# Moving the split weight buffers to other addresses in SBUF (a two-stage transformer layer in fp32r matmuls)

## The chip, the core and the metric

The kernel runs on one core of a Trainium2 chip. The metric is device time in microseconds (us), the median of three runs. Lengths of single instructions are given in nanoseconds (ns).

## What is computed

The reference is one layer of a hybrid encoder on an input of 256 tokens by 2048 features, in float32:

```python
u = rmsnorm(x, norm_mix_g)
z = u @ w_in                      # 2048 x 5140, four head groups
y = concat(gated_conv, pooling, gated_linear_attention, forgetting_attention)(z)
x = x + y @ w_out                 # 2048 x 2048
u = rmsnorm(x, norm_ffn_g)
x = x + (silu(u @ w_gate) * (u @ w_up)) @ w_down   # 2048 x 5632 twice, 5632 x 2048
```

The weights amount to some 50 million float32 numbers, each used once per run of the kernel.

## The kernel before

**Precision.** Each float32 operand is split into a high part, which is the value rounded to the format fp32r, and a low part, which is the rest. A product is then the sum of three: high times high, high times low and low times high. The activations u (for both norms), y (mixer output) and hT (hidden layer, 44 blocks of 128 features) are held in SBUF as such pairs, `u[:, k, 0]` the high and `u[:, k, 1]` the low part, 256 tokens each.

**Weights.** All big weights are packed into 384 chunks `wall[i]` of 128 partitions by 1024 columns (512 KB). `stage_through` (L104) brings a chunk from memory into one of four `raw` buffers, ScalarE rounds it into `hi` (L114) and VectorE subtracts to get `lo` (L115). There are four hi and four lo buffers, hi0 to hi3 and lo0 to lo3, and chunk i uses number i modulo 4. Chunks are prepared three ahead of the one in use (`LOOK`).

**Products.** Most chunks are used by `block_fm` (L136): 317 chunks, in which the weight is the stationary operand (128 by 128) and the activation is the moving one. Per chunk it does eight matmuls at L150 with `hi`, which stream both parts of the activation (512 columns), and eight at L155 with `lo`, which stream only the high part (256 columns). Eight matmuls alternate between two PSUM banks. In the last chunk of a block the eight of L155 come before the eight of L150. The first part of the program uses `block_lead` (L176, 256 columns at a time) and `block_tm` (L193), in which the weight chunk is the moving operand (512 columns) and the activation the stationary one. The last block (L159 to L171, `tail`) streams 256 columns per matmul.

**Order of the stages.** First 16 chunks in `block_lead` and `block_tm` for 40 chunks, until 163 us; then u times w_in by `block_fm` until 264 us; y times w_out until 353 us; gate and up projections (44 blocks of four chunks, so chunk 0 of a block always uses hi0 and lo0) until 843 us; then hT times w_down (eight blocks of eleven chunks, so that the buffer number and the place in the block are not tied), the eighth being the tail from 1056 us.

**Addresses.** Buffers lie in SBUF one behind the other, in the order in which the pools first see them. u begins at byte 32,896 of a partition. In what follows a buffer's *distance* is its address less that of u, modulo 512 bytes. A chunk buffer holds 4,096 bytes, but is allocated with 4,160 (`1040` columns, of which 1,024 are used), so each of the eight lies 64 bytes further on:

| buffer | hi0 | lo0 | hi1 | lo1 | hi2 | lo2 | hi3 | lo3 |
|---|---|---|---|---|---|---|---|---|
| distance from u before, bytes | 0 | 64 | 128 | 192 | 256 | 320 | 384 | 448 |

y and hT (which takes y's place later) begin at 125,568, a distance of 0 from u. Inside all these tensors each 128 by 128 weight begins at a multiple of 512 bytes and each activation part at a multiple of 1,024, so the distance holds for every matmul that pairs them.

Of the kernel before, what the change touches and what calls it, by code (L numbers as in the profile page):

```python
# [9 lines left out]
F32 = mybir.dt.float32  # L10
BF16 = mybir.dt.bfloat16
F32R = mybir.dt.float32r
# [5 lines left out]
P = 128  # L18
# [40 lines left out]
def trunk_kernel(ctx: ExitStack, tc: tile.TileContext, a, out):  # L59
# [4 lines left out]
    wpool = ctx.enter_context(tc.tile_pool(name="wpool", bufs=4))  # L64
    ev = ctx.enter_context(tc.tile_pool(name="ev", bufs=2))
# [31 lines left out]
    ones = con[:, C_ONE:C_ONE + P]  # L97


    staged = {}  # L100
    issued = [0]
    total = a["wall"].shape[0]

    def stage_through(n, ahead=AHEAD, parts=1):  # L104
        while issued[0] <= min(n, total - 1):
            i = issued[0]
            raw = wpool.tile([P, 1024], F32, name="raw", bufs=4)

            hi, lo = [wpool.tile([P, 1040], F32R, name=f"{v}{i % 4}", bufs=1)[:, :1024] for v in ("hi", "lo")]
            with tc.high_priority(offset=ahead):  # L110
                for q in range(parts):
                    c = slice(q * 1024 // parts, (q + 1) * 1024 // parts)
                    nc.sync.dma_start(out=raw[:, c], in_=a["wall"][i][:, c])
                    S.copy(out=hi[:, c], in_=raw[:, c])  # L114
                    V.tensor_tensor(out=lo[:, c], in0=raw[:, c], in1=hi[:, c].bitcast(F32), op=ALU.subtract)  # L115
            staged[i] = (hi, lo)
            issued[0] += 1
# [12 lines left out]
    def next_chunk():  # L130
        i = used[0]
        used[0] += 1
        stage_through(i + LOOK)
        return staged.pop(i)
# [91 lines left out]

    def rsqrt_of(dst, src, pool, mul, n):

        w = pool.tile([P, 64 if pool is ev else 3 * n], F32, name=f"rs{n}")
        v, r, q = [w[:, i * n:(i + 1) * n] for i in range(3)]  # L230
        V.tensor_scalar(out=v, in0=src, scalar1=mul, scalar2=EPS, op0=ALU.mult, op1=ALU.add)
        S.activation(out=r, in_=v, func=AF.Sqrt)
        V.reciprocal(out=r, in_=r)
        V.tensor_tensor(out=q, in0=r, in1=r, op=ALU.mult)
        V.scalar_tensor_tensor(out=q, in0=q, scalar=-0.5, in1=v, op0=ALU.mult, op1=ALU.mult)
        V.scalar_tensor_tensor(out=dst, in0=q, scalar=1.5, in1=r, op0=ALU.add, op1=ALU.mult)

    def token_rstd(sq):


        ps = misc()
        for t in range(2):
            PE.matmul(ps[:, t:t + 1], lhsT=sq[:, t * P:(t + 1) * P], rhs=con[:, C_ONE:C_ONE + 1], start=True, stop=True)
        rsqrt_of(rcol, ps[:, 0:2], ev, 1.0 / D, 2)
        yield
        yield
        ps2 = misc()
        for t in range(2):
            dg = ev.tile([P, P], F32, name="dg", bufs=1)
            V.tensor_scalar(out=dg, in0=ident, scalar1=rcol[:, t:t + 1], scalar2=None, op0=ALU.mult)  # L250
            PE.matmul(ps2[:, t * P:(t + 1) * P], lhsT=ones, rhs=dg, start=True, stop=True)
        S.copy(out=rb, in_=ps2[:, :T])
        yield
# [19 lines left out]
    for j in range(KT // 2):  # L273
        for ks in (slice(0, 1), slice(1, 2)) if j == 0 else (slice(2 * j, 2 * j + 2),):
            nc.sync.dma_start(out=xT[:, ks], in_=a["xT"][:, ks])
            if ks.start == 0:
                stage_through(0, 0, 2)
            for k in range(ks.start, ks.stop):
                split_u(k)
        stage_through(j, 0, 2)  # L280
# [187 lines left out]
    def gla_out(gv, sgg):  # L468
        ob = k4.tile([P, 2, 4, P], F32, name="ob", tag="k4")
        ss = mx.tile([P, 8], F32, name="gss")  # L470
        for t in range(2):
# [11 lines left out]
            yield  # L483
        rs = mx.tile([P, 8], F32, name="grs")
        rsqrt_of(rs, ss, mx, 1.0 / P, 8)
        for _ in range(8):
            yield
# [17 lines left out]
    def fox_qk(qk, qkT):  # L505

        ss = mx.tile([P, 16], F32, name="fss")
        for i in range(4):
            head_rstd(ss[:, 4 * i:4 * i + 4], qk[i // 2][:, i % 2].rearrange("p (h d) -> p h d", h=4), 4)
            yield  # L510
        rs = mx.tile([P, 16], F32, name="frs")
        rsqrt_of(rs, ss, mx, 1.0 / P, 16)
        for _ in range(3):
            yield
        for i in range(2):
            qn = k4.tile([P, 8, P], F32, name="qn", tag="k4")
            V.tensor_tensor(out=qn, in0=qk[i].rearrange("p t (h d) -> p (t h) d", h=4),
                            in1=rs[:, 8 * i:8 * i + 8, None].broadcast_to([P, 8, P]), op=ALU.mult)
            yield
            yield  # L520
            yield
            qT = k4.tile([P, 4, T], F32, name="qT", tag="k4")
            g = par[:, P_FQG + i:P_FQG + i + 1]
            for h in range(4):
                ps = misc()
                for t in range(2):
                    PE.transpose(out=ps[:, t * P:(t + 1) * P], in_=qn[:, t * 4 + h], identity=ident)
                if i == 0:
                    V.tensor_scalar(out=qT[:, h], in0=ps[:, :T], scalar1=g, scalar2=float(P) ** -0.5,
                                    op0=ALU.mult, op1=ALU.mult)  # L530
                else:
                    S.activation(out=qT[:, h], in_=ps[:, :T], func=AF.Copy, scale=g)
                yield
            qkT.append(qT)
# [175 lines left out]
    for j in range(2):  # L710
# [3 lines left out]
        for m in range(2):  # L714
            i = 2 * j + m
# [7 lines left out]
    for j in range(KT // 2):  # L723
        b = block_fm(y, order)
        for m in range(2):
            i = 2 * j + m
# [32 lines left out]
    for j in range(KT // 2):  # L759
        tail = j == KT // 2 - 1  # L760
        b = block_fm(hT, list(range(FT)), tail=tail)
        for m in range(2):
            i = 2 * j + m
# [65 lines left out]
```

## Time and profile before

| | us |
|---|---|
| median of three runs | 1093.26 (1093.09 to 1093.45) |
| the profiled execution's own time | 1092.44 |
| its span, first to last instruction | 1090.3 |
| TensorE matmul busy | 1084.9 |
| VectorE busy | 707.6 |
| ScalarE busy | 519.8 |

The profile's page gives busy times, a chain of the work that ended last, and groups of instructions. [...] What counts for the time is the spacing from one start to the next.

### The profile page before, as it was taken

How to read it: one execution, taken by the hardware profiler on the slowest of the kernel's cores; microseconds unless marked ns; L12 is line 12 of the kernel's file. 1: busy time of each engine (PE TensorE's matmuls, PEld its weight loads, DVE VectorE, ACT ScalarE, POOL GpSimd, SP SyncE). 2: the span in 40 equal slices, each digit the busy share in tenths (PEclk: the TensorE clock that was granted, in tenths of full speed). 3: DMA queues.
4: the chain of work that ended last, by engine and by line, in shares of the span. 5: the costliest groups of instructions: out<-in, count | busy, mean ns of one | idle time of the engine just before them, and what ended most of it. 6: DMA issues, size and time to landing. Idle time of an engine off the chain costs nothing.

```text
span 1090.3 us, 16159 instructions
## 1 busy us (share of the span) xinstructions
PE 1084.9 (100%) x6300; PEld 944.3 (87%) x6300; DVE 707.6 (65%) x996; ACT 519.8 (48%) x726; POOL 31.1 (3%) x35
## 2 busy tenths in 40 slices
PE   9999999999999999999999999999999999999998
PEld 8777878888888888888888888888888888888898
DVE  8798867886676766666666666666666544455542
ACT  8545555454544545454444545454544344433341
POOL 0000000000242100000000000000000000000000
PEclk9999999999999999999999999999999999999999
DMA  8654355555566566666666666656566666666661
GB/s 313 214 176 161 117 194 176 168 158 174 191 187 192 180 196 177 197 187 195 191 189 188 188 193 187 192 182 194 188 195 193 191 198 197 200 200 201 200 190 66
DMA packets 59724, 203.80 MB, mean 187 GB/s; under 512 B 6768, under 2 KB 9216, under 8 KB 59648
## 3 DMA queue, kind: packets, MB, share of 16 engines
q1 hardware_dynamic: 59504, 202.75, 60.0%
q8 instruction: 49, 0.80, 0.3%
q14 instruction: 27, 0.22, 0.1%
q10 hardware_dynamic: 144, 0.03, 0.0%
HBM read 200.65 MB, written 2.10 MB: 186 GB/s over the span
## 4 chain that ended last, share of the span: by engine, by line
PE 96%; ACT 2%; DVE 1%; DMA 1%; issue 0%; SPq 0%; DVEq 0%; ACTq 0%
PE acc L150 54%; PE acc L155 27%; PE acc L203 3%; PE acc L205 3%; PE acc L204 3%; PE acc L171 1%; PE acc L170 1%; PE acc L169 1%; PE misc L400 1%; ACT hi L114 1%; DMA raw<-in_wall 1%; ACT u L267 0%; DVE lo L115 0%; PE acc L661 0%; PE misc L564 0%
## 5 line engine op out<-in xcount | busy, mean ns | idle before, releaser
L115 DVE TENSOR_TENSOR lo<-raw,hi 128x1024 fp32r<-128x1024 f32 (+1 forms) x384 | 462.0, 1205 | 249.7 <-ACT hi L114 244.8
L114 ACT CAST hi<-raw 128x1024 fp32r<-128x1024 f32 (+1 forms) x384 | 395.8, 1032 | 351.2 <-PE acc L150 210.4
L150 PE MATMUL acc<-u,hi 128*128 128x512 f32 x1664 | 412.5, 394 | 0.0
L150 PEld LDWEIGHTS acc<-u,hi 128*128 128x128 f32 x1664 | 301.5, 188 | 58.1
L155 PEld LDWEIGHTS acc<-u,lo 128*128 128x128 f32 x1664 | 217.1, 188 | 12.6
L155 PE MATMUL acc<-u,lo 128*128 128x256 f32 x1664 | 221.2, 280 | 0.0
L150 PE MATMUL acc<-hT,hi 128*128 128x512 f32 x616 | 153.7, 393 | 0.0
L150 PEld LDWEIGHTS acc<-hT,hi 128*128 128x128 f32 x616 | 110.7, 188 | 20.8
L212 ACT COPY t<-acc 128x256 f32<-128x256 f32 x134 | 50.0, 373 | 158.2 <-PE acc L150 158.2
L214 DVE TENSOR_TENSOR t<-acc,t 128x256 f32<-128x256 f32 x134 | 56.3, 420 | 100.2 <-ACT t L212 99.9
L155 PEld LDWEIGHTS acc<-hT,lo 128*128 128x128 f32 x616 | 81.5, 188 | 5.7
L155 PE MATMUL acc<-hT,lo 128*128 128x256 f32 x616 | 82.7, 279 | 0.0
L203 PE MATMUL acc<-hi,u 128*128 128x512 f32 x160 | 64.3, 402 | 0.0
L205 PE MATMUL acc<-lo,u 128*128 128x512 f32 x160 | 63.1, 395 | 0.0
L150 PE MATMUL acc<-y,hi 128*128 128x512 f32 x256 | 63.0, 392 | 0.0
L204 PE MATMUL acc<-hi,u 128*128 128x512 f32 x160 | 63.0, 394 | 0.0
L150 PEld LDWEIGHTS acc<-y,hi 128*128 128x128 f32 x256 | 46.4, 188 | 9.0
L203 PEld LDWEIGHTS acc<-hi,u 128*128 128x128 f32 x160 | 30.0, 188 | 7.3
L205 PEld LDWEIGHTS acc<-lo,u 128*128 128x128 f32 x160 | 30.0, 188 | 6.9
L204 PEld LDWEIGHTS acc<-hi,u 128*128 128x128 f32 x160 | 30.1, 188 | 6.6 <-issue 0.3
L155 PEld LDWEIGHTS acc<-y,lo 128*128 128x128 f32 x256 | 33.3, 188 | 1.9
L155 PE MATMUL acc<-y,lo 128*128 128x256 f32 x256 | 33.8, 279 | 0.0
(197 smaller groups left out, 614.3 us busy)
## 6 DMA issues: line engine op xcount, KB each, us to landing
raw<-in_wall SPq DMA_DIRECT2D x368, 512.0 KB, 4.0
raw<-in_wall SPq DMA_DIRECT2D x16, 256.0 KB, 5.4
out_T<-t SPq DMA_DIRECT2D x16, 128.0 KB, 2.4
xT<-in_xT SPq DMA_DIRECT2D x7, 256.0 KB, 5.4
con<-in_con SPq DMA_DIRECT2D x1, 480.0 KB, 5.7
msk_raw<-in_msk SPq DMA_DIRECT2D x1, 448.0 KB, 5.6
xT<-in_xT SPq DMA_DIRECT2D x2, 128.0 KB, 3.0
poolw<-in_poolw SPq DMA_DIRECT2D x1, 256.0 KB, 3.9
```

Source lines behind the costliest of these rows:

```text
L114: S.copy(out=hi[:, c], in_=raw[:, c])
L115: V.tensor_tensor(out=lo[:, c], in0=raw[:, c], in1=hi[:, c].bitcast(F32), op=ALU.subtract)
L150: PE.matmul(b[m], lhsT=hi[:, kk, m * P:(m + 1) * P], rhs=rhs[:, order[c0 + kk]], start=c0 + kk == 0, stop=c0 + kk == n - 1)
L155: PE.matmul(b[m][:, T:], lhsT=lo[:, kk, m * P:(m + 1) * P], rhs=rhs[:, order[c0 + kk], 0], start=False, stop=False, skip_group_check=True)
L169: PE.matmul(o, lhsT=hi[:, kk, cs], rhs=rhs[:, k, 0], start=c0 + kk == 0, stop=False)
L170: PE.matmul(o, lhsT=hi[:, kk, cs], rhs=rhs[:, k, 1], start=False, stop=False)
L171: PE.matmul(o, lhsT=lo[:, kk, cs], rhs=rhs[:, k, 0], start=False, stop=c0 + kk == n - 1)
L203: PE.matmul(b[t], lhsT=u[:, k, 0, ts], rhs=hi[:, kk], start=k == 0, stop=False)
L204: PE.matmul(b[t], lhsT=u[:, k, 1, ts], rhs=hi[:, kk], start=False, stop=False)
L205: PE.matmul(b[t], lhsT=u[:, k, 0, ts], rhs=lo[:, kk], start=False, stop=k == KT - 1)
L212: S.copy(out=t1, in_=bank[:, T:])
L214: V.tensor_tensor(out=t2, in0=bank[:, :T], in1=t1, op=ALU.add)
```

## The change

The change gives the eight chunk buffers an explicit order and explicit gaps. It allocates the four `raw` buffers first, as before, and then a gap and a buffer of exactly 1,024 columns eight times; the `gap_...` tiles are never used. The scratch tile of `rsqrt_of` for the token norm becomes one buffer of 320 bytes in place of two of 256, which moves what is allocated after it.

```diff
+    def part(name):
+        return wpool.tile([P, 1024], F32R, name=name, bufs=1)
+
+    wpool.tile([P, 1024], F32, name="raw", bufs=4)
+    for name, gap in (("hi0", 16), ("lo0", 16), ("lo3", 8), ("hi1", 8), ("lo1", 16),
+                      ("hi2", 16), ("lo2", 16), ("hi3", 16)):
+        wpool.tile([P, gap], F32, name=f"gap_{name}", bufs=1)
+        part(name)
...
-            hi, lo = [wpool.tile([P, 1040], F32R, name=f"{v}{i % 4}", bufs=1)[:, :1024] for v in ("hi", "lo")]
+            hi, lo = [part(f"{v}{i % 4}") for v in ("hi", "lo")]
...
-        w = pool.tile([P, 64 if pool is ev else 3 * n], F32, name=f"rs{n}")
+        w = pool.tile([P, 80 if pool is ev else 3 * n], F32, name=f"rs{n}", bufs=1)
```

The distances become:

| buffer | hi0 | lo0 | lo3 | hi1 | lo1 | hi2 | lo2 | hi3 |
|---|---|---|---|---|---|---|---|---|
| distance from u after, bytes | 64 | 128 | 160 | 192 | 256 | 320 | 384 | 448 |

y and hT begin at 125,312 now, a distance of 256 from u; seen from them, each number of the table is 256 more or less. No instruction is added, removed or moved: on every engine both programs have the same instructions in the same order with the same waits, and only addresses differ.

## Rows read from the trace of the kernel before

**Rows 1.** The page: the span, the clock by slice, the last chain by engine.

```profile
span 1090.3 us, 16159 instructions
...
PEclk9999999999999999999999999999999999999999
...
PE 96%; ACT 2%; DVE 1%; DMA 1%; issue 0%; SPq 0%; DVEq 0%; ACTq 0%
```

**Rows 2.** The page's groups: matmuls of L150 and L155, count, busy, mean ns.

```profile
L150 PE MATMUL acc<-u,hi 128*128 128x512 f32 x1664 | 412.5, 394 | 0.0
...
L155 PE MATMUL acc<-u,lo 128*128 128x256 f32 x1664 | 221.2, 280 | 0.0
L150 PE MATMUL acc<-hT,hi 128*128 128x512 f32 x616 | 153.7, 393 | 0.0
...
L155 PE MATMUL acc<-hT,lo 128*128 128x256 f32 x616 | 82.7, 279 | 0.0
...
L150 PE MATMUL acc<-y,hi 128*128 128x512 f32 x256 | 63.0, 392 | 0.0
...
L155 PE MATMUL acc<-y,lo 128*128 128x256 f32 x256 | 33.8, 279 | 0.0
```

**Rows 3.** Waits of TensorE's matmuls: us in total, times, longest.

```profile
PE misc L263 <- DVE idle L259: 1.2, 1, 1.2
PE acc L186 <- ACT hi L114: 0.6, 1, 0.6
```

**Rows 4.** Timeline of one gate/up block: start us, us, instructions in a row.

```profile
620.37 2.21 PE L150 MATMUL acc<-u,hi 128*128 128x512 f32 x9
622.42 1.11 PE L155 MATMUL acc<-u,lo 128*128 128x256 f32 x8
623.37 2.02 PE L150 MATMUL acc<-u,hi 128*128 128x512 f32 x8
625.22 1.07 PE L155 MATMUL acc<-u,lo 128*128 128x256 f32 x8
626.13 2.00 PE L150 MATMUL acc<-u,hi 128*128 128x512 f32 x8
627.97 2.04 PE L155 MATMUL acc<-u,lo 128*128 128x256 f32 x16
629.85 2.02 PE L150 MATMUL acc<-u,hi 128*128 128x512 f32 x8
```

**Rows 5.** L150 inside the hi0, then the hi1 chunk: min/median/max ns.

```profile
L150 PE MATMUL acc<-u,hi x6: 389/389/389, 620.8 to 622.0; 128*128 128x512 f32 x6
L150 PE MATMUL acc<-u,hi x6: 392/395/398, 623.6 to 624.8; 128*128 128x512 f32 x6
```

**Rows 6.** L150, last of its chunk, before lo0 and before lo1: ns.

```profile
L150 PE MATMUL acc<-u,hi x1: 388/388/388, 622.2 to 622.2; 128*128 128x512 f32 x1
L150 PE MATMUL acc<-u,hi x1: 394/394/394, 625.0 to 625.0; 128*128 128x512 f32 x1
```

**Rows 7.** Matmuls of 256 columns: lead hi2, tail hi3, tail hi2, tail lo1.

```profile
L186 PE MATMUL acc<-u,hi x6: 283/283/283, 25.3 to 25.9; 128*128 128x256 f32 x6
L169 PE MATMUL acc<-hT,hi x8: 274/274/274, 1061.9 to 1064.3; 128*128 128x256 f32 x8
L169 PE MATMUL acc<-hT,hi x8: 281/281/283, 1059.1 to 1061.5; 128*128 128x256 f32 x8
L171 PE MATMUL acc<-hT,lo x7: 276/283/285, 1056.5 to 1058.6; 128*128 128x256 f32 x7
```

**Rows 8.** The 512-column matmuls of block_tm, moving hi and moving lo: ns.

```profile
L203 PE MATMUL acc<-hi,u x160: 387/393/498, 29.6 to 162.1; 128*128 128x512 f32 x160
L205 PE MATMUL acc<-lo,u x160: 388/394/483, 30.1 to 162.6; 128*128 128x512 f32 x160
```

**Rows 9.** Windows: us, busy PE, PEld, DVE, ACT, POOL, PEclk, DMA share, GB/s.

```profile
0.00:25.00 25.00, 23.24 (x165) 20.46 (x166) 20.76 (x38) 21.20 (x40) 0.20 (x4) 1.00 0.90 321
...
400.00:800.00 400.00, 400.00 (x2306) 351.08 (x2306) 255.42 (x361) 193.43 (x290) 0.00 (x0) 1.00 0.63 190
```

## Prediction

> **What bounds the kernel now.** I read the page first. One engine fills the span: TensorE, at 96% of the chain that ended last, on the upper clock level in every slice [rows 1]. The waits come next. TensorE waits 1.8 us for others in its two longest waits, both at the start [rows 3], so no transfer, rounding or subtraction sets the pace. The memory side has room: 321 GB/s in the first 25 us against 190 GB/s in the gate and up stage [rows 9]. What is left is how fast TensorE gets through its own queue, and most of that queue is 2536 matmuls of L150 and 2536 of L155 (1664 + 616 + 256 each) [rows 2].
>
> The change adds no instruction and moves none, so it can only act through the spacing of these matmuls. I therefore looked for whether equal matmuls are equally spaced, chunk by chunk, in the timeline of one gate and up block [rows 4]. Between the starts of the groups, divided by eight (sixteen where lo2 and lo3 stand in one row): hi1 from 623.37 to 625.22 is 232 ns a matmul, hi2 from 626.13 to 627.97 is 230 ns, lo0 from 622.42 to 623.37 is 118 ns, lo1 from 625.22 to 626.13 is 113.4 ns, lo2 and lo3 are 117.7 ns. hi0 is the most even: its recorded length is 389 ns in all six inner matmuls, while hi1 swings between 392 and 398 [rows 5]. [...] Shapes, order and banks are the same for hi0 and hi1; the buffer's address is not. That is the lever of the change.
>
> How length and spacing hang together: hi1's eight have a mean spacing of 232 ns at a mean length near 394, and lo1's 113.4 ns of spacing go with 276 recorded, so spacing is the recorded length less about 162 ns, within 2 ns. With that hi0's inner matmuls are 227 ns apart. I take the four hi buffers as 227, 232, 230 and 232 (hi3, from 629.85 to the start of the next block, is like hi1), mean **230.2 ns**; and lo as 118, 113.4, 117.7, 117.7, mean **116.7 ns**.
>
> While one matmul streams, the weights of the next are loaded. [...]
>
> **The hi parts (512 columns, distances 64, 192, 320, 448 after; 0, 128, 256, 384 now).** The last L150 of a hi chunk already loads from a lo buffer at such a distance: before lo0 (64) 388 ns, before lo1 (192) 394 ns [rows 6]. Before lo2 (320) it is 388 again, and in the last stage before lo3 (448) 394, so pairs 256 bytes apart read alike. Less 162 that is 226 and 232 ns, mean 229.0. Against 230.2 now: −1.2 ns × 2536 = **−3.0 us**. These are single matmuls that come out of a run of others, and hi0 shows that the first of a run is not like the rest, so the bounds are wide: all at 226 would be −4.2 ns × 2536 = −10.7 us, all at hi1's inner 395 − 162 = 233 would be +2.8 ns × 2536 = +7.1 us. I take the mean of the two rows since each stands for two of the four buffers.
>
> **The lo parts (256 columns, distances 128, 160, 256, 384 after; 64, 192, 320, 448 now).** Rows with 256 columns and such a distance are in the lead and in the tail (there L169 is followed by a load from the same hi, L171 by one from the next hi). At 256, hi2: 283 ns, steady, in the lead, 281 in the tail. At 384, hi3: 274 in the tail; at 128, hi1 loaded behind lo1: a median of 283 there [rows 7]. That is 121, 119, 112 and 121 ns of spacing. lo1 would stand at 256 (seen from y and hT at 0): 119 to 121 by these rows, but hi2's first load at 256 out of the lo1 run fits into 113.4 as well; I take 117. lo0 and lo2 stand at 128 and 384 and change places when y or hT streams: mean of 112 and 121, 116.5. For lo3 at 160, half way between two distances of the table, no row exists; I leave it at today's 116.7. Mean (117 + 116.5 × 2 + 116.7) / 4 = 116.7: **0**. The bounds are all at 112 (−4.7 × 2536 = −11.9 us) and all at 121 (+4.3 × 2536 = +10.9 us).
>
> **The rest.** In block_tm the chunk streams and u is loaded. L203, whose next load is at a distance that hi has now, has a median of 393 and L205, with the next load at one that lo has now, 394 [rows 8]: exchanging the two on 480 matmuls is worth 0, at most 1 ns × 480 = 0.5 us. Lead and tail have 456 matmuls of 256 columns with a mixture of both kinds of distance before and after: 0, within 4 ns × 456 = 1.8 us. The scratch of rsqrt_of becomes single, but it is used twice, some 300 us apart: 0. Rounding and subtracting write to other addresses too; both engines are off the chain and idle for a good part [rows 9], so even some per cent there would be covered by TensorE's queue.
>
> **Sum.** 1092.4 (the profiled execution's own time, 2.1 us above its span) −3.0 = 1089.4; the median of the runs shown is 0.8 us higher, so 1090.2. I take **1089**, one lower, since the bounds of hi lie further off below than above.
>
> [...] The rows show equal matmuls 6 ns apart by buffer alone [rows 5, 6]. [...]
>
> **Rivals.**
> 1. *The runs settle in a clean state.* hi0 keeps 389 for a whole run and lo1 276: such a run has no extra beyond 227 and 113.4 ns. If the new distances make every buffer do that, hi gains 3.2 and lo 3.3 ns: −16.5 us, 1077. For it: a run that is clean once stays so in these rows. Against it: 394 before lo1 and 283 in the lead show new pairs that are not clean. If only hi or only lo settles it is about 1085. Chance 0.14.
> 2. *The lo parts turn worse than the hi parts gain.* [...] In the lead such loads at distance 256 stay at 283 ns, 121 ns of spacing, with no sign of settling. If that holds for all four lo buffers, +10.9 − 3.0 = +7.9 us, 1101; with two of the four about 1096. It decides from a mean of lo above 116.7 + 1.2 = 117.9 ns. Against it: 274 in the tail at 384. Chance 0.28.
> 3. *The average stays.* Each of the two kinds of matmul takes over the other's kind of distance, and the sum could be the same within 2 us: 1093. For it: L203 and L205 differ by 1 ns only [rows 8]. Against it: [rows 6] lie below today's mean on average. Chance 0.16. [...]
>
> The forecast itself (hi somewhat faster, lo level) has 0.42, with its own range of 1085 to 1092.
>
> **Range and chances.** Faster by over 0.2% (below 1091.1; about what a measurement of this kernel can tell from no change) are nearly all of the forecast and rival 1: 0.55. Rival 3 and the edges of forecast and rival 2 are within 0.2%: 0.18. Slower: 0.27. The range of 1077 to 1102 ends at the clean state below and just above rival 2; it leaves out the sums of both good bounds (−22.6 us, 1071) and of both bad ones (+18 us, 1111).
>
> **What would show it.** In the changed kernel the timeline of a gate and up block should show its four hi groups at a mean of 229 ns and the four lo groups near 117; single chunks will lie apart, by pairs 256 bytes from each other (hi0 like hi2, hi1 like hi3). Inner matmuls of hi0 and hi2 should be near 388 and those of hi1 and hi3 near 394 if a single row tells of the run. Medians of L203 and L205 should stay at 393 and 394, and TensorE's waits below 3 us. The prediction is wrong if a whole run behaves unlike its first matmul (hi at 395 or above, or lo at 283 throughout), or if lo3 at 160 falls out of the pattern.

## The result and the profile after

The changed kernel takes 1102.12 us (median of four runs, 1101.65 to 1103.59) against 1093.17 for the kernel before on the same chip: a ratio of 1.0082, 95% interval 1.0069 to 1.0094. It is slower by 9 us. The profiled execution took 1101.65 us, with a span of 1099.6 us against 1090.3 [rows 1].

The page's groups answer to [rows 2] (L158 is L150 of before, L163 is L155; columns count, busy us, mean ns, idle):

```profile
span 1099.6 us, 16159 instructions
...
L158 PE MATMUL acc<-u,hi 128*128 128x512 f32 x1664 | 414.1, 395 | 0.0
...
L163 PE MATMUL acc<-u,lo 128*128 128x256 f32 x1664 | 224.7, 282 | 0.0
L158 PE MATMUL acc<-hT,hi 128*128 128x512 f32 x616 | 154.3, 394 | 0.0
...
L163 PE MATMUL acc<-hT,lo 128*128 128x256 f32 x616 | 84.7, 282 | 0.0
...
L158 PE MATMUL acc<-y,hi 128*128 128x512 f32 x256 | 63.3, 394 | 0.0
...
L163 PE MATMUL acc<-y,lo 128*128 128x256 f32 x256 | 34.3, 281 | 0.0
```

Busy time of the matmuls is up by 3.5 + 2.0 + 0.5 = 6.0 us in the low matmuls and by 1.6 + 0.6 + 0.3 = 2.5 us in the high ones: 8.5 of the 9.3 us of span. The rest is small pieces of the tail and of block_tm. TensorE's waits are almost as short as before (3.0 us in all against 2.4), so nothing new is waited for.

One gate and up block of the changed kernel on the timeline, which answers to [rows 4] (start us, us, instructions in a row):

```profile
624.69 2.26 PE L158 MATMUL acc<-u,hi 128*128 128x512 f32 x9
626.79 1.11 PE L163 MATMUL acc<-u,lo 128*128 128x256 f32 x8
627.74 2.01 PE L158 MATMUL acc<-u,hi 128*128 128x512 f32 x8
629.58 1.11 PE L163 MATMUL acc<-u,lo 128*128 128x256 f32 x8
630.53 2.03 PE L158 MATMUL acc<-u,hi 128*128 128x512 f32 x8
632.40 2.06 PE L163 MATMUL acc<-u,lo 128*128 128x256 f32 x16
634.30 2.00 PE L158 MATMUL acc<-u,hi 128*128 128x512 f32 x8
```

From start to start, hi1 is (629.58 − 627.74) / 8 = 230 ns a matmul and hi2 (632.40 − 630.53) / 8 = 234; lo0 is 119, lo1 119, lo2 and lo3 119. The records overlap: seven of hi1's matmuls are recorded at 388 to 397 ns. No low run at 113.4 is left. Inside the runs of hi0 and of lo1 (min/median/max ns):

```profile
L158 PE MATMUL acc<-u,hi x7: 392/393/398, 625.2 to 626.6; 128*128 128x512 f32 x7
L163 PE MATMUL acc<-u,lo x6: 283/283/283, 629.7 to 630.3; 128*128 128x256 f32 x6
```

hi0 at 64 swings between 393 and 398, where the single matmul of [rows 6] had 388. Where y streams, the two buffers that see 64 modulo 256 (hi0 and hi2) stand at 232.7 and 233.3 ns of spacing, the two that see 192 (hi1 and hi3) at 230.4 and 229.4. lo1 at 256 stays at 283: the lead's row for that distance [rows 7], not the 276 of its run before.

### The profile page after: what moved, and what is told of

Its sections match the earlier page's. It is cut to its first block, busy times and chain, and to the rows that moved or that the text cites. A ratio compares the mean times of both kernels' runs of the same rounds, so it can differ in the third digit from the quotient of the medians.

```text
span 1099.6 us, 16159 instructions
## 1 busy us (share of the span) xinstructions
PE 1093.5 (99%) x6300; PEld 950.3 (86%) x6300; DVE 707.6 (64%) x996; ACT 519.3 (47%) x726; POOL 31.1 (3%) x35
## 4 chain that ended last, share of the span: by engine, by line
PE 96%; ACT 2%; DMA 1%; DVE 1%; issue 0%; SPq 0%; DVEq 0%; ACTq 0%
PE acc L158 53%; PE acc L163 27%; PE acc L211 3%; PE acc L212 3%; PE acc L213 3%; PE acc L177 1%; PE acc L178 1%; PE acc L179 1%; DMA raw<-in_wall 1%; PE misc L408 1%; ACT hi L122 1%; ACT u L275 1%; DVE lo L123 0%; PE acc L669 0%; ACT sqp L302 0%
## 5 line engine op out<-in xcount | busy, mean ns | idle before, releaser
L158 PE MATMUL acc<-u,hi 128*128 128x512 f32 x1664 | 414.1, 395 | 0.0
L158 PEld LDWEIGHTS acc<-u,hi 128*128 128x128 f32 x1664 | 301.5, 188 | 59.0
L163 PEld LDWEIGHTS acc<-u,lo 128*128 128x128 f32 x1664 | 220.1, 189 | 13.3
L163 PE MATMUL acc<-u,lo 128*128 128x256 f32 x1664 | 224.7, 282 | 0.0
L158 PE MATMUL acc<-hT,hi 128*128 128x512 f32 x616 | 154.3, 394 | 0.0
L158 PEld LDWEIGHTS acc<-hT,hi 128*128 128x128 f32 x616 | 110.9, 188 | 20.9
L163 PEld LDWEIGHTS acc<-hT,lo 128*128 128x128 f32 x616 | 83.0, 189 | 6.1
L163 PE MATMUL acc<-hT,lo 128*128 128x256 f32 x616 | 84.7, 282 | 0.0
L158 PE MATMUL acc<-y,hi 128*128 128x512 f32 x256 | 63.3, 394 | 0.0
L158 PEld LDWEIGHTS acc<-y,hi 128*128 128x128 f32 x256 | 46.4, 188 | 9.1
L163 PEld LDWEIGHTS acc<-y,lo 128*128 128x128 f32 x256 | 33.8, 189 | 2.0
L163 PE MATMUL acc<-y,lo 128*128 128x256 f32 x256 | 34.3, 281 | 0.0
```

Source lines behind the costliest of these rows:

```text
L158: PE.matmul(b[m], lhsT=hi[:, kk, m * P:(m + 1) * P], rhs=rhs[:, order[c0 + kk]], start=c0 + kk == 0, stop=c0 + kk == n - 1)
L163: PE.matmul(b[m][:, T:], lhsT=lo[:, kk, m * P:(m + 1) * P], rhs=rhs[:, order[c0 + kk], 0], start=False, stop=False, skip_group_check=True)
```

## The experiments

In what follows a *run* is a row of matmuls of one kind out of one buffer, eight of them in most chunks, and it is called *clean* when it keeps the lowest spacing seen over a whole run (227 ns for hi, 113.4 for lo). Two theories are weighed again and again: A (later A'), that the distance sets the spacing of a run, and S, that the state in which the run begins decides it too.

All layouts below come from the same few lines (here those of lo new), with other gaps, and a last unused gap that keeps all that follows where it was before (y and hT at distance 0). Three runs leave the eight buffers alone: y, hT moved; no writers; order.

```diff
+    wpool.tile([P, 1024], F32, name="raw", bufs=4)
+    for name, gap in (("hi0", 0), ("hi1", 32), ("lo0", 0), ("lo3", 8), ("hi2", 24), ("lo1", 0), ("hi3", 32), ("lo2", 0), ("end", 32)):
+        if gap:
+            wpool.tile([P, gap], F32, name=f"gap_{name}", bufs=1)
+        if name != "end":
+            wpool.tile([P, 1024], F32R, name=name, bufs=1)
...
```

The table has all but the two runs that stream one kind of matmul only, which do other work. Medians are beside the kernel before on the same chip (1093.3 to 1093.6); hi and lo are the mean spacings in ns, worked out in each trace from the starts of all 2536 matmuls of a kind (a few long spacings are among them, 19 above 260 ns for hi in the kernel before, so hi reads about 1 ns more than in a single block). Means for one buffer are worked out in the same way.

| kernel | hi at | lo at | us | ratio, 95% | hi, ns | lo, ns |
|---|---|---|---|---|---|---|
| before | 0, 128, 256, 384 | 64, 192, 320, 448 | 1093.2 | | 231.4 | 116.8 |
| changed | 64, 192, 320, 448 | 128, 256, 384, 160 | 1102.1 | 1.0069 to 1.0094 | 232.4 | 119.1 |
| lo new | as before | as changed | 1103.2 | 1.0073 to 1.0103 | 232.3 | 119.8 |
| hi new | as changed | as before | 1095.7 | 1.0010 to 1.0029 | 232.6 | 116.9 |
| y, hT moved | as before | as before | 1093.4 | 0.9991 to 1.0010 | 231.5 | 116.8 |
| no writers | as before | as before | 1093.9 | one run | 231.5 | 116.8 |
| 0 and 192 | all 0 | all 192 | 1095.9 | 1.0013 to 1.0032 | 231.1 | 118.2 |
| 128 and 192 | all 128 | all 192 | 1100.8 | 1.0054 to 1.0088 | 233.4 | 117.2 |
| lo0, lo2 moved | as before | 192, 192, 448, 448 | 1097.2 | 1.0020 to 1.0046 | 231.4 | 118.0 |
| order | as before | as before | 1092.6 | 0.9991 to 1.0013 | 232.1 | 115.9 |
| odd 32 | 32, 96, 160, 224 | 96, 160, 224, 288 | 1106.8 | 1.0109 to 1.0135 | 234.2 | 118.8 |
| 192 and 64 | all 192 | all 64 | 1089.9 | 0.9955 to 0.9981 | 231.2 | 116.0 |
| 192 and 64, order | all 192 | all 64 | 1083.8 | 0.9901 to 0.9928 | 230.6 | 114.1 |
| 0 and 64, order | all 0 | all 64 | 1094.6 | 1.0004 to 1.0022 | 230.9 | 117.8 |

**Half of the change each.** The diff is the loop above (lo new), and with `("hi0", 16), ("lo0", 0), ("hi1", 32), ("lo1", 0), ...` for hi new.

> hi buffers at the distances of before (0, 128, 256, 384), lo buffers at those of the change (128, 256, 384, lo3 160), y and hT at 0 as before. Theory A (the spacing belongs to the pair of moving tensor and next weights, so hi and lo cost separately): the mean spacing of the L155-type matmuls goes from 116.7 to about 119.1 ns as in the changed kernel, the hi ones stay at 231: +6 us, 1099. Theory B (it is the place of the hi and lo buffers against each other, or of all tensors together): the loss does not divide; hi and lo both move, and the time is anywhere near 1093 or 1102, but not the sum of its parts. Theory C (the shift of y and hT by 256 bytes): 1093.

> hi buffers at the distances of the change (64, 192, 320, 448), lo buffers at those of before (the same four numbers), y and hT at 0. Theory A: the hi matmuls go from 231 to about 232 ns of spacing, lo stays near 116.7: +2.5 us, 1096. Theory B: not the rest of what the exchange of the lo buffers alone costs. Theory C: 1093.

Hi alone costs 2.3 us, as theory A had it. But the mean of lo stays level only by cancellation: where u streams, lo1 goes from 113.7 to 117.8 ns and lo0 from 118.1 to 116.1, though no lo buffer changed its distance. Lo alone costs 9.7 us, not 6: lo rises by 3.0 ns (7.5 us), and the hi matmuls rise by 0.9 ns too, though no hi buffer changed its distance. The two halves sum to 12.0 us where the whole costs 9.0. So the low parts carry most of it, but the terms do not add, as theory B had it: what a run costs depends on its neighbours.

**The shift of y and hT.**

```diff
-        w = pool.tile([P, 64 if pool is ev else 3 * n], F32, name=f"rs{n}")
+        w = pool.tile([P, 64 if pool is ev else 3 * n], F32, name=f"rs{n}", bufs=1)
```

> The buffers of before; only the scratch of the token norm becomes one buffer of 256 bytes, which puts y and hT at a distance of 256 from u. Theory A with a period of 256 bytes: 1093, and every chunk's spacing as before. Theory C (this shift is what cost): up to +9 us, all of it in the stages that stream y and hT.

The time is the same, and in each of the 24 pairs of buffer and streamed tensor the mean spacing is within 0.3 ns of before. Moving the streamed tensor by 256 bytes changes nothing, and theory C falls.

**Without the writers.** Chunks from 96 on are neither loaded nor split:

```diff
+            if i >= 96:
+                staged[i] = last[i % 4]
+                issued[0] += 1
+                continue
...
```

> The kernel before, with chunks 96 to 383 neither loaded nor rounded nor subtracted: their matmuls read what buffers 0 to 3 hold from chunks 92 to 95 (the result is not the reference's). Same addresses, same matmuls. Theory A: the spacing is TensorE's two reads against each other, so every chunk keeps its spacing (hi 227, 232, 230, 232, lo 118, 113.4, 117.7, 117.7). [...]

There are 376 chunks, not 384, the last being 375: the page's `raw<-in_wall` rows are 368 whole chunks and 16 halves of the first eight, and these eight, not 16, are what `block_lead` uses. From 400 to 800 us, where the DMA of before moves 190 GB/s [rows 9], no weights are loaded now, and yet the mean spacings are those of before to 0.1 ns (231.5 and 116.8, one run). So loads, rounding and subtracting account for 0.1 ns of the spacing at most.

What makes the spacings differ, no run shows. The address of the weights alone is not all: in block_tm the weights always come from u, and only the address of the streamed chunk changes with the layout. The same line (L204 of before) with all hi at 128 and lo at 192, then with all hi at 192 and lo at 64:

```profile
L210 PE MATMUL acc<-hi,u x160: 387/390/497, 30.3 to 163.2; 128*128 128x512 f32 x160
L210 PE MATMUL acc<-hi,u x160: 388/394/497, 30.6 to 163.2; 128*128 128x512 f32 x160
```

The medians are 390 and 394 ns. Whether it is TensorE's two reads against each other, as theory A has it, no run shows. No run moves u, y and hT against each other by anything but 256 bytes, so in `block_fm` the distance of a weight buffer is not told apart from its own address.

**The two clean distances everywhere, and the clean pair four times.** Layouts `("hi0", 0), ("hi1", 0), ("hi2", 0), ("hi3", 0), ("lo0", 48), ("lo1", 0), ...`, and the same from 128 on.

> All four hi buffers at distance 0, all four lo buffers at 192, y and hT at 0: the two distances at which a whole run had no extra in the kernel before (hi0 227 ns, lo1 113.4 ns). Theory A with runs that settle: hi 227 and lo 113.4 ns throughout, -17 us, 1076. Rival: what a run costs is decided by the state in which it begins, not by its distance; the mean stays and the time is 1088 to 1098.

> All hi at 128, all lo at 192: the pair hi1 and lo1 of the kernel before, four times over. Theory A' with the run before it counted in (lo at 192 is clean behind hi at 128): hi 232.5, lo 113.4 ns, 1088 to 1090. Theory S: the clean lo runs also needed what stood before hi1; lo at 118, 1095 to 1099.

With 0 and 192 the clean lo run does not come: the time is 1095.9, as the rival had it, and lo1 stands near 118 ns in all 52 blocks that stream u. With 128 and 192 the time is 1100.8, above even theory S's 1099, since hi at 128 stands at 233.4 ns when every chunk has it. lo1 is clean there in 24 of its 52 runs where u streams, and for most of the gate and up stage in every second block. Inner matmuls of lo1 in the kernel before, then in two blocks of the kernel with 128 and 192, one after the other:

```profile
L155 PE MATMUL acc<-u,lo x6: 276/276/276, 625.3 to 625.9; 128*128 128x256 f32 x6
```

```profile
L161 PE MATMUL acc<-u,lo x6: 279/279/280, 629.1 to 629.7; 128*128 128x256 f32 x6
L161 PE MATMUL acc<-u,lo x7: 276/276/276, 640.3 to 640.9; 128*128 128x256 f32 x7
```

The two blocks have the same addresses, the same order and the same hi run ahead, and yet they differ by 3 to 4 ns a matmul. So these three do not settle what a run costs; what else does, these blocks do not show.

**Long runs of one kind.** High only: L155's eight are left out, and four more with hi take their place. Low only: the high matmuls are left out but in a block's first chunk, and in the other chunks the low ones are done three times. Each was run once (1091.60 and 1115.55 us).

> Leaves the products with the low parts of the weights out of all four-row chunks but the tail and streams the high parts 12 times a chunk instead of 8; hi0 to hi3 at 0, 64, 128, 192, y and hT at 0. Long runs of 512-column matmuls, only the distance differs. [...]

> Leaves the products with the high parts out of all chunks but the first of a block and does those with the low parts three times; lo0 to lo3 at 0, 64, 128, 192. Long runs of 256-column matmuls. Theory A': lo at 0 120 ns (the 283 ns of recorded length of the lead), at 64 116 to 118, at 128 119 to 120, at 192 113.4 to 118 ns. Theory S: lo at 192 is 113.4 behind some chunks and 117.8 behind others, and the rest is not ordered by distance.

High only, inner matmuls at 0, 64, 128 and 192, in the stage that streams hT:

```profile
L156 PE MATMUL acc<-hT,hi x6: 389/389/395, 953.2 to 954.3; 128*128 128x512 f32 x6
L156 PE MATMUL acc<-hT,hi x6: 393/396/398, 955.9 to 957.1; 128*128 128x512 f32 x6
L156 PE MATMUL acc<-hT,hi x6: 390/394/404, 958.7 to 959.9; 128*128 128x512 f32 x6
L156 PE MATMUL acc<-hT,hi x6: 388/392/394, 950.5 to 951.6; 128*128 128x512 f32 x6
```

Means of a chunk's eight in that stage are 228.0, 233.3, 232.1 and 228.9 ns: for 512 columns the distance sorts the runs here, as theory A' said, and 64 is the worst of the four, not the best. Low only, two runs at 64 bytes, one where u and one where hT streams:

```profile
L161 PE MATMUL acc<-u,lo x22: 281/281/281, 762.8 to 765.3; 128*128 128x256 f32 x22
L161 PE MATMUL acc<-hT,lo x21: 276/276/276, 966.5 to 968.8; 128*128 128x256 f32 x21
```

For 256 columns this one distance has more than one steady run: over twenty matmuls in a row at 281, or over twenty at 276. Both kinds come in one stage: where hT streams, 8 of the 18 long runs at 64 are at 276 and 10 at 281. At 0, 128 and 192 the medians are 283, 281 and 279, near theory A'. So the distance does not settle what a run at 64 costs, nor one at 192 (279 here, 276 for lo1 in the kernel before), as theory S said. Each theory is half right.

**Moving only what stands ahead of the clean run.** Layout as before, lo0 to 192 and lo2 to 448.

> The kernel before with only lo0 and lo2 moved, from 64 to 192 (modulo 256); hi0 to hi3 and lo1, lo3 stay where they were. Theory S (a run can keep the state in which it begins; lo1 was clean because its hi1 run began behind a lo run at 64): lo1 and, where hT streams, lo3 lose their 113.4 ns and go to 116 to 118 though neither they nor hi1 and hi3 moved; about +3 us, 1096 to 1097. Theory A' (distance, and the run directly before): lo1 stays at 113.4, lo0 and lo2 stay near 118: 1093 to 1094.

Theory S holds: 1097.2 us, lo1 at 117.7 ns in place of 113.7. lo1 and lo3 have the very addresses of before; hi1 and hi3 lie 4,096 bytes lower, at the same distance. Inner matmuls of lo1 answer to the 276 above:

```profile
L161 PE MATMUL acc<-u,lo x6: 279/279/280, 628.0 to 628.6; 128*128 128x256 f32 x6
```

**The order in a block's last chunk.**

```diff
-                for f in (rest, whole) if c0 + 4 == n else (whole, rest):
+                for f in (whole, rest):
```

> No address changes: in the last chunk of a block the eight high matmuls come before the eight low ones, as in the other chunks. Theory S: in the stages that stream u and y each chunk then begins as where hT streams, so lo3 falls from 117.7 to 113.4 ns, and hi0, which then begins behind a lo run, rises from 227 to 229.5: -2.1 and +1.2 us, 1092 to 1093. Theory A': nothing changes in any chunk, 1093.5.

By the profile theory S holds: in the stage that streams y, lo3 goes from 117.7 to 113.3 ns and hi0 from 227.1 to 229.9. By the time it is undecided: of twelve runs eight took 1091.5 to 1092.7 us, as expected, and four 1095.7 to 1096.8. The profiled one is of the eight; what the four do is not known.

**Other distances.** Layouts `("hi0", 8), ("hi1", 16), ("lo0", 0), ("hi2", 16), ...` and `("lo0", 16), ("lo1", 0), ("lo2", 0), ("lo3", 0), ("hi0", 32), ("hi1", 0), ...`.

> Distances that are odd multiples of 32 bytes: hi 32, 96, 160, 224, lo 96, 160, 224, 32 (modulo 256). If only the 64-byte step counts, an odd multiple is like its neighbour and the mean spacings stay within 231 to 233 and 117 to 119.5 ns: 1094 to 1102. If half steps are a kind of their own (lo3 at 160 in the changed kernel, 118 to 120 ns, is the one row), some chunk lies outside of all that the 64-byte distances gave.

> All hi at 192, all lo at 64: of the long runs measured alone the second best for hi (229 ns) and the best for lo (116 to 118 ns). Theory A': hi 229 to 230, lo 116.5: 1089 to 1092. Theory S: another entry than in the long runs, hi at 231 to 232 and lo at 117 to 118, as with hi at 192 and lo at 192 in the run with only hi moved: 1094 to 1097.

Odd multiples of 32 are worse for hi than every layout of 64-byte steps that was tried (234.2 ns against 230.6 to 233.4; 1106.8 us); lo stays within what was expected. All hi at 192 with all lo at 64 is faster than before, as A' forecast and S did not. Its stages show two steady runs again, lo0 where u and where hT streams:

```profile
L161 PE MATMUL acc<-u,lo x6: 280/281/281, 622.5 to 623.1; 128*128 128x256 f32 x6
L161 PE MATMUL acc<-hT,lo x5: 276/276/276, 954.6 to 955.1; 128*128 128x256 f32 x5
```

Distances and code of the two are the same; but where u streams, every block of four chunks begins after a chunk in swapped order (low before high), and where hT streams only every block of eleven. That made a forecast possible: take the swap out.

> All hi at 192 and all lo at 64, and high before low in every chunk. Theory S (entry and distance together): with one distance each and one order, the stages that stream u and y have the entry of the stage that streams hT, so their chunks take its spacings, hi 229.8 and lo 114.7 in place of 231.9 and 116.4 ns: 240 chunks x 8 x 3.8 ns = -7 us against the kernel with these distances alone, 1083. Theory A' (distance alone decides): no change in any chunk, 1090.

> All hi at 0 and all lo at 64, high before low in every chunk. Theory S: lo as behind hi at 0 in the kernel before, 118 ns; hi at 0 behind lo at 64 has no row, as long runs 228, behind a lo run 229.5 to 230: 1092 to 1094. Theory A' (the distances that are best each by itself are best together): hi 228, lo 116, 1087.

The first takes 1083.8 us, 0.85% below the kernel before, as theory S had it (1083). The chunks of its gate and up block are now alike:

```profile
628.17 2.00 PE L156 MATMUL acc<-u,hi 128*128 128x512 f32 x8
630.01 1.07 PE L161 MATMUL acc<-u,lo 128*128 128x256 f32 x8
630.92 2.00 PE L156 MATMUL acc<-u,hi 128*128 128x512 f32 x8
632.76 1.07 PE L161 MATMUL acc<-u,lo 128*128 128x256 f32 x8
633.67 2.00 PE L156 MATMUL acc<-u,hi 128*128 128x512 f32 x8
635.50 1.07 PE L161 MATMUL acc<-u,lo 128*128 128x256 f32 x8
```

That is 230 ns for hi and 114 for lo in each. The second, made of each kind's best distance in long runs, has lo at 117.8 everywhere and takes 1094.6, a little above theory S's 1092 to 1094 and far from A''s 1087. In these two runs a distance was good only together with what stood before it: lo at 64 has 114.1 ns with hi at 192 and 117.8 with hi at 0.

## Why the prediction was wrong

**What bounds the kernel** was right: no wait worth naming appeared, and 8.5 of the 9.3 us of span lie in the spacing of the two kinds of matmul. That addresses alone move them was right as well: the layouts differ in nothing else. The two that lie furthest apart with one order of instructions differ by 17 us (1106.8 and 1089.9); what waits there, no run shows. That a shift by 256 bytes changes nothing is shown for y and hT (0.3 ns at most), and without the loads the mean spacings moved by 0.1 ns at most.

**The step on the hi parts failed.** It read the cost of a run from one matmul, the last of its chunk, which loads from a buffer at the new distance [rows 6]. The load itself is in the trace of before: the first weights from lo0 are loaded from 622.20 us on, while the last L150 streams, and their own matmul starts at 622.42; in the median a load starts 227 ns ahead of its matmul for L150 and 115 ns for L155. But that the recorded length of this one matmul gives the spacing of a whole run at the distance of the buffer that follows, which the −3.0 us of the sum rests on, no run shows. The prediction itself said that the first of a run is not like the rest, and then used it with both ends as bounds. The run at 64 is not 388 but 393 and 398 in turn, 233 ns of spacing in place of 226, and the runs at 192 are at 230.4 and 229.4 ns, where y streams, in place of 232: the two rows gave the wrong order of the two distances. In place of −3.0 us the hi parts cost +2.5 us (hi alone measured +2.3).

**The step on the lo parts failed too, by a choice between rows.** It had the right row, the lead's steady 283 at 256, and mixed it with the tail's and with a last-of-run matmul to 117. It also took 121 ns at 128 and 112 at 384, though it had just read pairs 256 bytes apart as alike; lo0 and lo2, at those two distances, both came out at 119. lo1 came out at the lead's value inside its run, and all four low buffers at about 119 ns: +6.0 us in place of 0. A second part was not seen at all: lo1 was not clean by its distance alone. In the run with lo0 and lo2 moved, these two stayed at 118, and the whole rise of lo from 116.8 to 118.0 is in lo1 and, where hT streams, in lo3, which had not moved (lo1 117.7 for 113.7 where u streams). A clean run was lost here by what was put ahead of it.

**The rest** was put at 0 and is the other 0.8 us of span; the median of L203 went from 393 to 396.

**Rival 2** named the right place and the lead's right row. Its price was too high for lo (+10.9 against 6.0) and it kept the hi gain of 3.0, which was a loss of 2.5; that its total of 1101 lies near the result is partly chance. **The sum** of separate terms is itself a wrong step: the halves measured singly make 12.0 us, the whole 9.0.

What remains open: whether a run keeps a state from its beginning, and which, whether it is the distance or the weights' own address that counts, and why the kernel with the new order alone has two times. These are described here, not explained.

## What to carry to other kernels

Where a matmul stream is the bound, compare equal matmuls buffer by buffer: if their spacings differ, other addresses are worth a trial. Here the layouts, two of them with another order in a block's last chunk, lie 2% apart (1083.8 to 1106.8 us). A layout could not be priced here from single matmuls (−3.0 us forecast for hi, +2.5 measured) or from runs out of their surroundings (hi at 0 and lo at 64, the best in the long runs, took 1094.6 us where theory A' had 1087); take steady runs of the same surroundings, or measure. Making all chunks alike (one distance for each kind, one order) made one steady run hold in both layouts that were tried, with lo at 114.1 and at 117.8 ns, but which one had to be measured: hi at 192 with lo at 64 gave 0.85% here, hi at 0 with lo at 64 in the same order lost 0.1%. Moving eight buffers by hand to eight places lost 0.8%.

## What was not expected of the hardware

Low matmuls of one shape, in one order, with the weights at a distance of 64 from the moving tensor, ran steadily in two ways over more than twenty matmuls in a row, recorded at 276 or at 281 ns; with hi at 128 and lo at 192, lo1 took turns from block to block, at 276 and 279. Taking the low-before-high order out of a block's last chunk, with no address changed, moved lo3 from 117.7 to 113.3 ns where y streams. Shifting the streamed tensor by 256 bytes changed no buffer's mean spacing by more than 0.3 ns, and distances of odd multiples of 32 bytes were the worst for 512 columns (234.2 ns in the mean against 231.1 in the best layout of the same order).
